# Branch gates and branch outputs as separate units of work, a shorter chain of mixers, and opening loads in another order, in a two-layer decoder trunk

## The chip, the cores and the metric

The kernel runs as one program on one core of one Trainium2 chip. The metric is the device time of one execution in microseconds (us); the kernel before takes 2546.94 us, the median of three runs. In the text PE is TensorE (matmuls), ACT is ScalarE, DVE is VectorE, POOL is GpSimd, and SP is the engine whose queue issues the DMAs. A matmul of 512 columns takes its place on PE for about 0.227 us (43.53 us for 192 in a row, in the chain of work of the profile).

## The reference, cut to what matters

512 tokens of width 1024 pass through two layers. Each layer is a half-step SwiGLU FFN, a block of four parallel token mixers, and a second half-step FFN. The block that the change touches:

```
h  = rmsnorm(x);  z = h @ w_in           # q, k, v and gates of four mixers
outs = (diff_attention, mlstm, stick_breaking, dsa)      # four mixers, each 512 x 256
y  = sum over b of sigmoid(gate_b) * (outs[b] @ w_branch[b])    # gate_b is 512 x 1024
x  = x + y @ w_out
```

`dsa` picks the 256 best keys of each query by a learned index score. `mlstm` needs input and forget gates. All is computed in float32; a product is made of three fp32r matmuls of high and low parts.

## The kernel before, in words

All tensors lie with features on the 128 partitions and the 512 tokens along the free dimension. A weight tile of 128 x 1024 is split into a high and a low part (`weights()`), and each 128 x 128 block of it multiplies a tile `xh`/`xl` of the input three times (`mm3`). A projection of one output tile is 8 blocks, so 24 matmuls of 512 columns.

The FFNs are plain loops. The mixer block (`mixers()`) is different. One long chain of small steps, `heads()`, runs the mixers one after the other: stick-breaking, the index of dsa, mlstm, differential attention, dsa. A step issues some score matmuls (tiles `S`), and ACT and DVE work on the scores. Later `weigh_steps` transposes the weights of a head (tiles `T`) and multiplies them with the values (tile `A`). Beside this chain stands a list of *units*: projections and branch units, all with many full matmuls into tiles `g`. A small planner (`run()`, `fill()`) keeps a clock of the PE work issued so far. A chain step says how long its results will take (`yield SB_US`, `yield DIFF_US` and so on); until that much PE work has been issued, the planner issues pieces of units, the first unit in the list whose `needs` are done. When no unit can go, the planner issues the next chain step at once. The scheduler of the framework then fixes one order for each engine, and each engine runs its own order strictly.

In the kernel before, `branch_unit` holds both a gate projection and the branch output that it multiplies, for two of the eight output tiles, and it needs the finished mixer (`o_sb`, `o_ml`, `o_diff`, `o_dsa`):

```
def push_branch(name, pairs, *needs):
    for i in pairs:
        push(f"{name}{i}", branch_unit(name, i), ("o_" + name, *needs))
```

The 512-wide half tiles of branch weights take a place in the same ring of three places, `w`, as the 1024-wide tiles. Weights of the sb and ml gates and branches have been split ahead and come back from DRAM as high and low parts (`w<-ig` 1 MB, `w<-br` 0.5 MB); those of diff and dsa come raw (`w_raw`) and are split on ACT and DVE when used.

At the opening, SP loads the small table, the first x tile, two whole weight tiles of the second FFN column (`w_raw`), and then the pieces `raw` of the first column.

Of the kernel before, what the change touches and what calls it, by code (L numbers as in the profile page):

```python
# [39 lines left out]
for _n, _w in (("ident", 128), ("mean", 128), ("bo32", 128), ("bo64", 128), ("cum", 128), ("cols", 12),  # L40
               ("ones", 128), ("m_qk", 128), ("m_kq", 128), ("m_strict", 128), ("sel", 1024), ("selp", 256)):
    CB[_n] = (_off, _w)
    _off += _w
# [11 lines left out]
NSMALL = _off  # L55
# [7 lines left out]
IDX_US, SB_US, DIFF_US, ML_US, DSA_US = 1.89, 2.64, 3.5, 3.96, 4.46  # L63
FIRST_US, LAST_US, WEIGH_US, NORM_US, SPREAD_US, STACK_US = 7.92, 5.41, 3.0, 2.88, 9.2, 9.84
GATE_US, SELECT_US, HALF_US, DEN_US, REST_US, KV_US, OUT_US = 0.7, 6.29, 6.75, 1.24, 8.76, 1.49, 1.0
# [5 lines left out]
GB, SB_, TB, AB = 3, 2, 2, 1  # L71
BRANCH = {"diff": 0, "ml": 1, "sb": 2, "dsa": 3}
# [3 lines left out]
def trunk_kernel(ctx, tc, xT, pos, consts, small, wgu1, wdn1, wgu2, wdn2, wia, wig, wiv, wbr, wout, out,  # L76
# [44 lines left out]

    def weights(src, n, key=None, c=0):

        with tc.high_priority(offset=WPRI):
            if key in ready:
                w = w_tile()
# [4 lines left out]
            w = w_tile()  # L131
# [55 lines left out]
    for l in range(depth):  # L187
        t = cpool.tile([P, NSMALL], F32, name=f"small{l}")
        sms.append(t)
# [22 lines left out]
    def open_sums():  # L212
        sums["pool"] = ExitStack()
        p = sums["pool"].enter_context(tc.tile_pool(name="sums", bufs=1, side="right", reuse_waits="tile"))
        sums["sum"], sums["tmp"] = [p.tile([P, T], F32, name=f"rsum{i}") for i in range(2)]
# [24 lines left out]
    def rms_rows(psum):  # L240
# [6 lines left out]
        r = cpool.tile([P, T], F32, name="rrow")  # L247
# [186 lines left out]
    def mixers(l, y, mp, kp, pp, psT, psS):  # L434
# [19 lines left out]
        tasks, units, done, unit, before = [], [], {}, [None], [None]  # L454
        issued.clear()
        live = {"z": 0, "a": 0, "o": 0, "ot": 0, "norm": 0}
# [21 lines left out]
        def fill():  # L478
            if unit[0] is None:
                u = next((u for u in units if all(n in done for n in u.needs) and (not u.z or live["z"] < 3)), None)  # L480
                if u is None:
                    return False
                units.remove(u)
                live["z"] += u.z
                unit[0] = u.gen
# [30 lines left out]
        def push(name, gen, needs=(), z=0):  # L516
            units.append(SimpleNamespace(name=name, gen=gen, needs=needs, z=z))
# [56 lines left out]
        def branch_unit(name, pair):  # L574

            b = BRANCH[name]
            for i in (2 * pair, 2 * pair + 1):
                half, n = divmod(i, 4)
                w = weights(wig[l, b * KD + i], 1024, ("ig", l, b * KD + i))
                ps = gpool.tile([P, T], F32, name="g")  # L580
                yield from proj_steps(w, ps)
                g = tmp("gate", 2)
                with tc.high_priority(offset=EVPRI):
                    tanh_half(g, ps)
                if n % 2 == 0:
                    o = 512 * (n // 2)
                    bw = weights(wbr[l, b, half, :, o:o + 512], 512, ("br", l, b, half), o)
                yield
                ps = gpool.tile([P, T], F32, name="g")
                for k in range(2):  # L590
                    mm3(ps, *bw((2 * (n % 2) + k) * P), *done["o_" + name][k], k == 0, k == 1)
                with tc.high_priority(offset=EVPRI):
                    V.scalar_tensor_tensor(g if i in started else y[i], g, 1.0, ps, op0=OP.add, op1=OP.mult)
                    if i in started:
                        (V if b == BRANCH["dsa"] else G).tensor_add(y[i], y[i], g)
# [4 lines left out]
                if i % 2 == 0:  # L600
# [3 lines left out]
        def push_branch(name, pairs, *needs):  # L604
            for i in pairs:
                push(f"{name}{i}", branch_unit(name, i), ("o_" + name, *needs))
# [190 lines left out]

        def sparse_kv(z):
# [29 lines left out]
        push_branch("sb", (0,))  # L828
        push("vm", v_unit("m"), ("o_sb",))
        push_branch("sb", (1,))  # L830
        push_branch("sb", (2,), "gated")
        push_branch("sb", (3,), "gated", "ml0")
# [4 lines left out]
        push_branch("ml", (0, 1))  # L837
        push_proj("fq1", ("diff0",), after=diff_q)
        push_proj("fk1", ("diff0",), after=diff_k)
        push_branch("ml", (2,))  # L840
# [3 lines left out]
        push_branch("ml", (3,))  # L844
        push_branch("diff", range(4))
        push_branch("dsa", range(4))
# [67 lines left out]

        def gating():
# [23 lines left out]
            yield lambda: "index" in done  # L939
# [18 lines left out]
            V.tensor_scalar(mst[:, :T], f32(selr[:, 0]), 0.0, None, op0=OP.mult)  # L958
            V.tensor_scalar(mst[:, T:], f32(selr[:, 0, :P]), 0.0, None, op0=OP.mult)
# [21 lines left out]
            V.tensor_scalar(est, f32(selr[:, 0]), 0.0, None, op0=OP.mult)  # L981
# [51 lines left out]
        def differential():  # L1033
            lamt = mp.tile([P, 4], F32, name="lamt")
            for i in range(2):
                t_ = mp.tile([P, 32], F32, name="lp", bufs=2)
                lp = sm(l, "lam")
                V.tensor_mul(t_, lp[:, 64 * i:64 * i + 32], lp[:, 64 * i + 32:64 * i + 64])
                V.reduce_sum(lamt[:, i:i + 1], t_, axis=AX.X)
            S.activation(lamt[:, :2], lamt[:, :2], AF.Exp)  # L1040
            V.tensor_sub(lamt[:, 2:3], lamt[:, 1:2], lamt[:, 0:1])
            V.tensor_scalar(lamt[:, 2:3], lamt[:, 2:3], -lam_init, None, op0=OP.add)
# [41 lines left out]
        def mlstm():  # L1084
            yield from get("gated")
            mv, mvl = yield from need("vm")
            yield lambda: not weighing
            for h in range(4):
# [5 lines left out]
                else:  # L1094
                    spawn(*((stacks(0), "stk0") if pr else (halves(("mq1", twice), ("mk1", both)), "ml1")))
# [304 lines left out]
```

## Time and profile before

| | |
|---|---|
| median of 3 runs | 2546.94 us (2545.94 to 2547.75) |
| the profiled execution | 2546.6 us, span 2544.8 us |
| PE | 98% of the span busy, 11584 matmuls |
| DVE / ACT / POOL | 58% / 39% / 6% |
| granted PE clock over the span | 0.987 of full |

The profile shows PE busy nearly always, and the share of busy time of a pipelined engine overstates its work. What can be won stands in the stretches where PE is less than full or where its granted clock is below 1. The mixer block of layer 0 lies from about 376 to 880 us, that of layer 1 from about 1640 to 2143 us. In the tables by stretch the second number in a column is the number of instructions, and PEclk is the mean granted clock of the stretch (1.00 is 2.4 GHz, 0.50 is 1.2 GHz).

### The profile page before, as it was taken

How to read it: one execution, taken by the hardware profiler on the slowest of the kernel's cores; microseconds unless marked ns; L12 is line 12 of the kernel's file. 1: busy time of each engine (PE TensorE's matmuls, PEld its weight loads, DVE VectorE, ACT ScalarE, POOL GpSimd, SP SyncE). 2: the span in 40 equal slices, each digit the busy share in tenths (PEclk: the TensorE clock that was granted, in tenths of full speed). 3: DMA queues.
4: the chain of work that ended last, by engine and by line, in shares of the span. 5: the costliest groups of instructions: out<-in, count | busy, mean ns of one | idle time of the engine just before them, and what ended most of it. 6: DMA issues, size and time to landing. Idle time of an engine off the chain costs nothing.

```text
span 2544.8 us, 30625 instructions
## 1 busy us (share of the span) xinstructions
PE 2496.6 (98%) x11584; PEld 2043.2 (80%) x11584; DVE 1481.8 (58%) x2664; ACT 983.7 (39%) x1556; POOL 154.6 (6%) x104
## 2 busy tenths in 40 slices
PE   8999999999989999999999999999999899999999
PEld 6888888778667888888888888887777678888887
DVE  7655557895465554343565655479954754444433
ACT  5434434633345332232343444345323543322222
POOL 1000010001012010000100000100011120100000
PEclk9999999999989999999999999999999899999999
DMA  8999966544521423323289999464555124232332
GB/s 293 321 324 331 334 237 205 156 152 156 168 68 63 139 93 100 99 92 99 91 311 319 339 327 330 153 224 126 176 164 165 34 80 135 96 99 93 99 99 91
DMA packets 113026, 444.11 MB, mean 175 GB/s; under 512 B 14704, under 2 KB 15984, under 8 KB 90352
## 3 DMA queue, kind: packets, MB, share of 16 engines
q1 hardware_dynamic: 112880, 442.16, 51.6%
q8 instruction: 91, 1.49, 0.2%
q14 instruction: 55, 0.45, 0.1%
HBM read 320.47 MB, written 102.76 MB: 166 GB/s over the span
## 4 chain that ended last, share of the span: by engine, by line
PE 87%; DVE 7%; DMA 2%; ACT 2%; issue 1%; POOL 0%; SPq 0%; DVEq 0%; ACTq 0%; POOLq 0%
PE g L102 43%; PE d L102 18%; PE u L102 18%; PE S L102 3%; PE A L102 1%; PE T L108 1%; DVE scores L902 1%; DMA w<-ig 1%; DVE m L901 1%; PE T L102 1%; DVE w L133 1%; DVE rl L93 0%; DMA stk<-stk 0%; DVE z L700 0%; ACT w L132 0%
## 5 line engine op out<-in xcount | busy, mean ns | idle before, releaser
L102 PE MATMUL g<-xh,w 128*128 128x512 f32 x3008 | 1001.7, 398 | 11.4 <-DMA w<-ig 5.6
L102 PEld LDWEIGHTS g<-xh,w 128*128 128x128 f32 x3008 | 570.2, 190 | 129.9 <-DVE stk L93 5.3
L132 ACT ACTIVATE w<-w_raw 128x1024 fp32r<-128x1024 f32 (+1 forms) x334 | 339.4, 1019 | 705.5 <-PE g L102 249.2
L102 PE MATMUL g<-xl,w 128*128 128x512 f32 x1504 | 594.4, 395 | 0.3 <-DVE xl L96 0.3
L133 DVE TENSOR_TENSOR w<-w_raw,w 128x1024 fp32r<-128x1024 f32 (+1 forms) x334 | 395.2, 1185 | 109.2 <-ACT w L132 109.0
L102 PE MATMUL u<-xh,w 128*128 128x512 f32 x1408 | 454.5, 390 | 0.5 <-DVE w L93 0.5
L102 PE MATMUL d<-hh,w 128*128 128x512 f32 x1408 | 435.6, 389 | 0.2 <-ACT hh L92 0.2
L102 PEld LDWEIGHTS g<-xl,w 128*128 128x128 f32 x1504 | 285.9, 190 | 56.4 <-DVE xl L96 1.1
L102 PEld LDWEIGHTS u<-xh,w 128*128 128x128 f32 x1408 | 264.6, 188 | 55.4 <-DVE w L93 0.9
L102 PEld LDWEIGHTS d<-hh,w 128*128 128x128 f32 x1408 | 264.3, 188 | 55.2 <-ACT hh L92 0.6
L102 PE MATMUL d<-hl,w 128*128 128x512 f32 x704 | 274.1, 389 | 0.2 <-DVE hl L93 0.2
L102 PE MATMUL u<-xl,w 128*128 128x512 f32 x704 | 274.1, 389 | 0.0
L171 DVE TENSOR_TENSOR a_w<-a_raw,a_w 128x1024 fp32r<-128x1024 f32 x92 | 112.5, 1223 | 112.9 <-ACT a_w L170 112.6
L337 DVE SCALAR_TENSOR_TENSOR x<-d,x 128x512 f32<-128x512 f32 x96 | 66.3, 691 | 190.3 <-PE d L102 190.3
L287 DVE TENSOR_TENSOR u<-u,rrow 128x512 f32<-128x512 f32 x88 | 60.7, 689 | 170.1 <-PE u L102 170.1
L170 ACT ACTIVATE a_w<-a_raw 128x1024 fp32r<-128x1024 f32 x92 | 97.3, 1059 | 154.9 <-DMA a_raw<-in_wig_dram 65.5
L102 PEld LDWEIGHTS d<-hl,w 128*128 128x128 f32 x704 | 132.1, 188 | 28.3 <-DVE hl L93 0.8
L102 PEld LDWEIGHTS u<-xl,w 128*128 128x128 f32 x704 | 132.4, 188 | 27.4
L225 POOL TENSOR_TENSOR rsum<-rsum,rsum 128x512 f32<-128x512 f32 x42 | 67.5, 1607 | 1234.8 <-ACT rsum L223 1234.8
L285 DVE TENSOR_TENSOR t<-g,rrow 128x512 f32<-128x512 f32 x88 | 60.7, 690 | 114.5 <-PE g L102 109.0
L102 PE MATMUL S<-stk 128*128 128x384 f32 (+3 forms) x304 | 94.0, 369 | 15.8 <-ACT p L713 8.4
L102 PE MATMUL g<-oh,w 128*128 128x512 f32 x256 | 93.6, 404 | 0.5 <-ACT gate L688 0.5
(262 smaller groups left out, 2602.7 us busy)
## 6 DMA issues: line engine op xcount, KB each, us to landing
w_raw<-in_wgu_dram SPq DMA_DIRECT2D x174, 512.0 KB, 3.8
ia<-a_w SPq DMA_DIRECT2D x40, 1024.0 KB, 6.6
w<-ia SPq DMA_DIRECT2D x40, 1024.0 KB, 5.4
w_raw<-in_wdn_dram SPq DMA_DIRECT2D x64, 512.0 KB, 4.1
ig<-a_w SPq DMA_DIRECT2D x32, 1024.0 KB, 6.9
w<-ig SPq DMA_DIRECT2D x32, 1024.0 KB, 5.9
a_raw<-in_wia_dram SPq DMA_DIRECT2D x40, 512.0 KB, 6.8
a_raw<-in_wig_dram SPq DMA_DIRECT2D x32, 512.0 KB, 7.2
```

Of the source, the lines that this page charges most:

```text
L102: ins = PE.matmul(out, a, b, start=start, stop=stop, skip_group_check=True)
L108: PE.transpose(out, a, C("ident")[p:n, p:n])
L132: S.activation(w[:, 0, :n], raw[:, :n], AF.Copy)
L133: V.tensor_sub(w[:, 1, :n], raw[:, :n], f32(w[:, 0, :n]))
L170: S.activation(w[:, 0], raw, AF.Copy)
L171: V.tensor_sub(w[:, 1], raw, f32(w[:, 0]))
L225: G.tensor_add(sums["sum"], sums["sum"], sums["tmp"])
L285: V.tensor_mul(t, pg, r)
L287: V.tensor_mul(u, pu, r)
L337: V.scalar_tensor_tensor(x[i], ps, 0.5, x[i], op0=OP.mult, op1=OP.add)
L901: V.max(out=m8, in_=s)
L902: V.match_replace(out=s, in_to_replace=m8, in_values=s, imm_value=TAKEN)
```

## The change

PE's work stays the same matmuls (one more warming matmul at the start). What changes:

- `branch_unit` becomes `gate_unit` (24 matmuls, tanh, result in a place) and `out_unit` (12 matmuls for two output tiles). A gate needs no mixer, only a place: for sb the first four go into `y`, for diff six go into the tiles of mlstm's values (`stash`), the others into a ring of four tiles `gate` (before: two). `fill()` avoids two out units in a row while another unit can go (`resting`).
- The half tiles of branch weights get a place of their own, `wb`, one tile; the three places `w` hold only 1024-wide tiles.
- The planner's numbers change (the waits after a chain step are shorter).
- The chain is shorter: `gating` no longer waits for the index, `mlstm` no longer waits at its end for its last output, the second half of mlstm's q and k is asked for at its start, and lambda of the differential attention is computed at the start of the block from a load of its own.
- At the opening the pieces of the first column are loaded before the tiles of the second, with high priority.
- Constants shrink (`sel` 1024 to 8 columns, `lam` out of the small table), and `rrow` moves to the pool of the sums.

```
-IDX_US, SB_US, DIFF_US, ML_US, DSA_US = 1.89, 2.64, 3.5, 3.96, 4.46
+IDX_US, SB_US, DIFF_US, ML_US, DSA_US = 1.5, 2.4, 3.0, 3.3, 4.0
...
+    def w_half():
+        return wpool.tile([P, 2, 512], FR, name="wb", bufs=1)
...
-                u = next((u for u in units if all(n in done for n in u.needs) and (not u.z or live["z"] < 3)), None)
-                if u is None:
+                able = [u for u in units if all(n in done for n in u.needs)
+                        and (not u.z or live["z"] < 3) and (not u.g or live["g"] < GATES)]
+                if not able:
                     return False
+                u = next((u for u in able if not (u.out and resting[0])), able[0])
...
-        def branch_unit(name, pair):
+        def gate_unit(name, i, place):
             b = BRANCH[name]
-            for i in (2 * pair, 2 * pair + 1):
...
+            w = weights(wig[l, b * KD + i], 1024, ("ig", l, b * KD + i))
+            ps = gpool.tile([P, T], F32, name="g")
+            yield from proj_steps(w, ps)
+            g = place()
+            with tc.high_priority(offset=EVPRI):
+                tanh_half(g, ps)
+            done[f"g_{name}{i}"] = g
+
+        def out_unit(name, pair, ring):
+            b = BRANCH[name]
+            half, o = pair // 2, 512 * (pair % 2)
+            bw = weights(wbr[l, b, half, :, o:o + 512], 512, ("br", l, b, half), o)
+            for n, i in enumerate((2 * pair, 2 * pair + 1)):
+                g = done[f"g_{name}{i}"]
                 ps = gpool.tile([P, T], F32, name="g")
                 for k in range(2):
-                    mm3(ps, *bw((2 * (n % 2) + k) * P), *done["o_" + name][k], k == 0, k == 1)
+                    mm3(ps, *bw((2 * n + k) * P), *done["o_" + name][k], k == 0, k == 1)
...
+        def push_gates(name, tiles, place=None, needs=()):
+            for i in tiles:
+                push(f"g_{name}{i}", gate_unit(name, i, place or (lambda: tmp("gate", GATES))), needs, g=int(not place))
...
-        push_branch("diff", range(4))
-        push_branch("dsa", range(4))
+        for p in range(3):
+            push_gates("diff", (2 * p, 2 * p + 1), stash, ("mlo1",))
+            push_outs("diff", (p,), ring=())
+        push_gates("diff", (6, 7))
+        push_outs("diff", (3,))
+        for p in range(4):
+            push_gates("dsa", (2 * p, 2 * p + 1))
+            push_outs("dsa", (p,))
...
-            yield lambda: "index" in done
             yield GATE_US
...
+            spawn(halves(("mq1", twice), ("mk1", both)), "ml1")
             yield lambda: not weighing
...
-            yield from get("mlo1")
...
-        for i in range(8):
+        for i in range(9):
             PE.matmul(ps, idle[:, :P], idle, start=True, stop=True, skip_group_check=True)
...
-    with tc.tile_pool(name="first", bufs=1, reuse_waits="tile") as rp:
+    with tc.tile_pool(name="first", bufs=1, reuse_waits="tile") as rp, tc.high_priority(offset=2 * WPRI):
```

First place: PE, layer 0, where dsa's first head starts. `S` are score tiles, `mask,identb` adds a mask, `g<-x..,w` are matmuls of a gate or projection. Before:

```order
L102 MATMUL S<-mask,identb 128x384
L102 MATMUL S<-stk 128x512 x2
L102 LDWEIGHTS identb
L102 MATMUL S<-mask,identb 128x512
L102 MATMUL S<-stk 128x128 x2
L102 LDWEIGHTS identb
L102 MATMUL S<-mqk,identb 128x128
L102 MATMUL S<-stk 128x256 x2
L102 LDWEIGHTS identb
L102 MATMUL S<-mask,identb 128x256
L102 MATMUL S<-stk 128x384 x2
L102 LDWEIGHTS identb
```

The scores of six steps stand there one right behind the other. Now, at the same scores of the same heads:

```order
L104 MATMUL S<-mqk,identb 128x128
L104 MATMUL g<-xl_82,w 128x512
L104 MATMUL g<-xh_74,w 128x512
L104 MATMUL g<-xh_75,w 128x512
L104 MATMUL g<-xl_83,w 128x512
L104 MATMUL g<-xh_75,w 128x512
L104 MATMUL S<-stk 128x256 x2
L104 LDWEIGHTS identb
L104 MATMUL S<-mask,identb 128x256
L104 MATMUL g<-xh_76,w 128x512
L104 MATMUL g<-xl_84,w 128x512
L104 MATMUL g<-xh_76,w 128x512
```

Five gate matmuls stand between the scores of one step and the next, and nine behind that.

Second place: PE, layer 0, the first two outputs of the ml branch. `oh_5543` is a finished half of the mixer's output, `w_5523` and `wb_5547`, `wb_5676` are half tiles of branch weights. Before, behind the first output of a pair:

```order
L102 MATMUL g_5610<-oh_4951,w_5523 128x512
L102 MATMUL S_5438<-stk_5269,stk_5259 128x128
L102 LDWEIGHTS identb_89
L102 MATMUL S_5438<-mqk_90,identb_89 128x128
L102 MATMUL g_5610<-ol_4952,w_5523 128x512
L102 MATMUL g_5610<-oh_4951,w_5523 128x512
L102 MATMUL g_5610<-oh_5422,w_5523 128x512
L102 MATMUL g_5610<-ol_5423,w_5523 128x512
L102 MATMUL g_5610<-oh_5422,w_5523 128x512
L102 MATMUL g_5621<-xh0_71,w_5619 128x512
```

A gate (`w_5619`) follows the last matmul with the half tile. Now:

```order
L110 MATMUL T_5534<-cst_67,tmp_5413 128x128 x4
L104 MATMUL g_5549<-oh_5543,wb_5547 128x512
L104 MATMUL g_5558<-oh_5543,wb_5547 128x512
L104 MATMUL g_5549<-ol_5544,wb_5547 128x512
L104 MATMUL g_5549<-oh_5543,wb_5547 128x512
L104 MATMUL g_5558<-ol_5544,wb_5547 128x512
L104 MATMUL g_5558<-oh_5543,wb_5547 128x512
L104 MATMUL S_5569<-stk_5293,stk_5283 128x512
L104 LDWEIGHTS identb_89
```

Right behind these nine rows come a second score step of 512 columns, eight small matmuls of tiles `T`, and then the first matmul with the next half tile, `wb_5676`, in the same single place. The four transposes at the head of the piece, which the output `oh_5543` is made from, have moved to directly ahead of it.

Third place: SP's queue at the very start. `x` are input tiles, `raw` the pieces of the first FFN column, `w_raw` the tiles of the second. Before:

```order
L1213 DMA small0_87<-in_small_dram 128x186
L1214 DMA x0_104<-in_xT_dram 128x512
L130 DMA w_raw_255<-in_wgu1_dram 128x1024
L130 DMA w_raw_260<-in_wgu1_dram 128x1024
L1231 DMA raw0_132<-in_wgu1_dram 128x256
L1231 DMA raw1_133<-in_wgu1_dram 128x256
```

The pieces come fifth and sixth, behind 1 MB of tiles. Now:

```order
L1279 DMA raw0_134<-in_wgu1_dram 128x256
L1261 DMA small0_87<-in_small_dram 128x58
L1279 DMA raw1_135<-in_wgu1_dram 128x256
L1262 DMA x0_105<-in_xT_dram 128x512
L1275 DMA x1_106<-in_xT_dram 128x512
L1275 DMA x2_107<-in_xT_dram 128x512
```

The tiles `w_raw` have moved behind the last of the x tiles, to the eighteenth place.

## Rows read from the trace of the kernel before

**Rows 1.** The page: busy time, share of the span and instructions by engine.
```profile
PE 2496.6 (98%) x11584; PEld 2043.2 (80%) x11584; DVE 1481.8 (58%) x2664; ACT 983.7 (39%) x1556; POOL 154.6 (6%) x104
```

**Rows 2.** Stretches, layer 0: length, busy PE, PEld, DVE, ACT, POOL; PEclk, DMA share, GB/s.
```profile
0.00:25.00 25.00, 19.28 (x64) 12.28 (x65) 15.87 (x20) 14.31 (x27) 8.73 (x10) 0.93 0.81 288
...
410.00:473.00 63.00, 63.00 (x364) 53.36 (x363) 47.25 (x92) 33.08 (x68) 5.21 (x3) 1.00 0.64 197
473.00:507.00 34.00, 30.98 (x192) 25.83 (x190) 32.50 (x91) 21.35 (x48) 1.08 (x3) 1.00 0.39 122
507.00:600.00 93.00, 91.53 (x447) 73.84 (x446) 79.74 (x230) 31.99 (x62) 0.00 (x0) 1.00 0.45 151
600.00:640.00 40.00, 38.68 (x184) 31.13 (x182) 23.08 (x66) 10.33 (x19) 8.88 (x6) 0.96 0.53 163
640.00:700.00 60.00, 55.43 (x257) 41.95 (x258) 31.14 (x85) 23.95 (x66) 5.51 (x4) 0.94 0.55 164
700.00:750.00 50.00, 46.50 (x231) 36.72 (x229) 33.39 (x105) 21.09 (x47) 7.52 (x5) 0.93 0.25 79
750.00:780.00 30.00, 25.67 (x118) 18.34 (x117) 22.69 (x60) 22.59 (x57) 5.54 (x4) 0.77 0.08 27
```

**Rows 3.** By stretch, the same parts of layer 1.
```profile
1736.00:1770.00 34.00, 30.96 (x191) 25.83 (x190) 32.47 (x90) 21.33 (x48) 1.08 (x3) 1.00 0.38 120
1770.00:1863.00 93.00, 91.01 (x445) 73.43 (x445) 79.42 (x228) 32.14 (x62) 0.00 (x0) 1.00 0.45 152
1863.00:1903.00 40.00, 39.10 (x186) 31.57 (x184) 23.53 (x67) 10.33 (x19) 8.92 (x6) 0.96 0.51 161
1903.00:1963.00 60.00, 55.74 (x259) 42.20 (x260) 31.69 (x86) 23.96 (x66) 5.51 (x4) 0.94 0.55 168
1963.00:2013.00 50.00, 46.72 (x228) 37.03 (x227) 33.03 (x104) 20.86 (x47) 7.41 (x5) 0.90 0.24 75
2013.00:2043.00 30.00, 25.68 (x117) 18.28 (x117) 22.73 (x60) 22.50 (x56) 5.67 (x4) 0.77 0.09 27
```

**Rows 4.** Waits of PE, 395 to 840 us: total, times, longest.
```profile
PE S L102 <- ACT p L713: 4.2, 6, 1.1
...
PE g L102 <- DMA w<-ig: 2.2, 1, 2.2
```

**Rows 5.** PE in order of time: a dsa score step and what ended its wait.
```profile
759.53 0.80 PE L102 MATMUL S<-stk 128*128 128x256 f32 x2 [1.14 <-ACT p L713]
```

**Rows 6.** By stretch, a piece inside the differential heads, columns as in rows 2.
```profile
643.50:646.90 3.40, 3.40 (x11) 2.32 (x10) 2.87 (x9) 1.53 (x6) 1.27 (x1) 0.50 0.45 103
```

**Rows 7.** Chain of waits: start, us, what.
```profile
101.96 43.53 PE d L102 x192
```

**Rows 8.** DMA issues: count, KB each, median us from issue to landing.
```profile
w<-br SPq DMA_DIRECT2D x16, 512.0 KB, 4.7
```

**Rows 9.** ACT in order of time: an output half made in layer 0.
```profile
623.16 0.63 ACT L92 ACTIVATE oh<-ot 128x512 fp32r<-128x512 f32 x1 [5.18 <-DVE ot L1140]
```

**Rows 10.** DVE in order of time: the steps ahead of that half.
```profile
621.66 0.74 DVE L628 SCALAR_TENSOR_TENSOR ot<-ot,mhg,T 128x512 f32<-128x512 f32 x1
...
622.44 0.69 DVE L1140 SCALAR_TENSOR_TENSOR ot<-z,ot 128x512 f32<-128x512 f32 x1
```

**Rows 11.** All engines in order of time: the opening.
```profile
1.18 0.42 SPq L1214 DMA_DIRECT2D x<-in_xT_dram  x1
...
1.64 0.91 SPq L130 DMA_DIRECT2D w_raw<-in_wgu_dram  x2
...
4.30 0.72 ACT L95 ACTIVATE xh<-x,small 128x512 fp32r<-128x512 f32 x1 [2.07 <-DMA x<-in_xT_dram]
...
7.60 0.42 ACT L92 ACTIVATE w<-raw 128x256 fp32r<-128x256 f32 x1 [2.05 <-DMA raw<-in_wgu_dram]
...
8.07 0.50 PE L102 MATMUL g<-xh,w 128*128 128x512 f32 x1 [3.26 <-ACT w L92]
```

More of the change, by code (lines that the diff above doesn't have):

```diff
@@ L187, in trunk_kernel @@
     for l in range(depth):
-        t = cpool.tile([P, NSMALL], F32, name=f"small{l}")
+        t = cpool.tile([P, NMAIN], F32, name=f"small{l}")
         sms.append(t)
@@ L214, in open_sums @@
         p = sums["pool"].enter_context(tc.tile_pool(name="sums", bufs=1, side="right", reuse_waits="tile"))
-        sums["sum"], sums["tmp"] = [p.tile([P, T], F32, name=f"rsum{i}") for i in range(2)]
+        sums["sum"], sums["tmp"], sums["row"] = [p.tile([P, T], F32, name=n) for n in ("rsum", "square", "rrow")]
     def epilogue(i, gain):
@@ L246, in rms_rows @@
         rsqrt_columns(ps, NT, v, y, t)
-        r = cpool.tile([P, T], F32, name="rrow")
+        r = sums["row"]
         spread(r.rearrange("p (t f) -> p t f", t=NT), y[:, :, None], P)
@@ L450, in blk @@
             return slice(i * P, i * P + n)
-        tasks, units, done, unit, before = [], [], {}, [None], [None]
+        tasks, units, done, unit, before, resting = [], [], {}, [None], [None], [False]
         issued.clear()
-        live = {"z": 0, "a": 0, "o": 0, "ot": 0, "norm": 0}
+        live = {"z": 0, "a": 0, "o": 0, "ot": 0, "norm": 0, "g": 0}
         def spawn(gen, key=None):
@@ L514, in take, with push @@
             live[what] += 1
-        def push(name, gen, needs=(), z=0):
-            units.append(SimpleNamespace(name=name, gen=gen, needs=needs, z=z))
+        def push(name, gen, needs=(), z=0, g=0, out=False):
+            units.append(SimpleNamespace(name=name, gen=gen, needs=needs, z=z, g=g, out=out))
         def proj_steps(w, ps):
@@ L594, in branch_unit @@
                     if i in started:
-                        (V if b == BRANCH["dsa"] else G).tensor_add(y[i], y[i], g)
+                        (V if name == "dsa" else G).tensor_add(y[i], y[i], g)
+                live["g"] -= i in ring
                 started.append(i)
@@ L796, in mixers @@
             V.tensor_scalar(gains[n], sm(l, n), -s / 8192, None, op0=OP.mult)
+        lamt, lp = mp.tile([P, 4], F32, name="lamt"), tmp()
+        nc.sync.dma_start(lp[:, :128], small[l, :, NMAIN:])
+        for i in range(2):
+            o = 64 * i
+            V.tensor_mul(lp[:, 128 + o:160 + o], lp[:, o:o + 32], lp[:, o + 32:o + 64])
+            V.reduce_sum(lamt[:, i:i + 1], lp[:, 128 + o:160 + o], axis=AX.X)
+        S.activation(lamt[:, :2], lamt[:, :2], AF.Exp)
+        V.tensor_sub(lamt[:, 2:3], lamt[:, 1:2], lamt[:, 0:1])
+        V.tensor_scalar(lamt[:, 2:3], lamt[:, 2:3], -lam_init, None, op0=OP.add)
         def sparse_kv(z):
@@ L827, in mixers @@
             push_proj(n, func=silu_conv(i))
-        push_branch("sb", (0,))
+        for i in range(4):
+            push_gates("sb", (i,), lambda i=i: y[i], (f"sb{i // 2}",))
+        push_outs("sb", (0,), ring=())
         push("vm", v_unit("m"), ("o_sb",))
-        push_branch("sb", (1,))
-        push_branch("sb", (2,), "gated")
-        push_branch("sb", (3,), "gated", "ml0")
+        push_gates("sb", (4, 5))
+        push_outs("sb", (1,), ring=())
+        push_gates("sb", (6, 7))
+        push_outs("sb", (2,), "gated")
+        push_outs("sb", (3,), "gated", "ml0")
         push_proj("mo0", ("ml0",), func=tanh_half)
@@ L1094, in mlstm @@
                 else:
-                    spawn(*((stacks(0), "stk0") if pr else (halves(("mq1", twice), ("mk1", both)), "ml1")))
+                    if pr:
+                        spawn(stacks(0), "stk0")
                 acc = psA()
```

77 lines of the change are left out of this document (37 added, 40 removed).

## The prediction

> **What bounds the kernel now.** I read the page first, then the table by stretch, then the waits of PE, then single places in order of time. On the page PE is busy for 98% of the span, DVE for 58%, ACT for 39% [rows 1], and the change leaves PE the same matmuls. So nothing can be won but the time in which PE has no matmul, or runs them at half clock.
>
> The tables by stretch show where that is. In a stretch of length W with PE busy B and mean granted clock c, the loss is (W - B) + (1 - c) x W: the first part is idle, the second is work that a clock at half speed (1.2 instead of 2.4 GHz) did not do. Layer 0 [rows 2]: 410 to 473 loses nothing (63.00 busy of 63.00, clock 1.00). 473 to 507 loses 3.0, with DVE busy 32.50 of 34. 507 to 600 loses 1.5; 600 to 640 loses 1.3 + 1.6 = 2.9; 640 to 700 loses 4.6 + 3.6 = 8.2; 700 to 750 loses 3.5 + 3.5 = 7.0; 750 to 780 loses 4.3 + 6.9 = 11.2. Together 33.8 us. Layer 1, the same six stretches [rows 3]: 3.0, 2.0, 2.5, 7.9, 8.3 and 11.2, together 34.9 us. The opening, 0 to 25, loses 5.7 + 1.75 = 7.5 us [rows 2]. That is 76 us in all; the FFNs lose next to nothing.
>
> Why they are lost: from 640 to 780 the chain of mixers (differential attention, then dsa) is alone or nearly alone on PE. A score step waits for the ACT exponential that frees its PSUM tile: six waits, 4.2 us in all, in layer 0 [rows 4], for example 1.14 us at 759.53 [rows 5]. The units that could stand between need `o_diff` or `o_dsa`, which the chain has yet to make. Half clock stands behind such waits, as in 643.5 to 646.9, where PE is busy all the time and the clock is 0.50 [rows 6]. One gate waits 2.2 us for its weights [rows 4], since the half tiles hold places of the ring of three.
>
> **Opening.** Now the first real matmul waits at 8.07 for the piece `raw`, which ACT gets at 7.60 although x was there at 4.30 [rows 11]: 1 MB of `w_raw` is issued ahead of it, at 1.64. The transfer of x takes 4.30 - 1.18 = 3.1 us. In the new order x is fourth; with 0.45 us for each issue (0.91 for two) it is issued at about 2.1, lands at 5.2, and ACT needs 0.72: first matmul at about 5.9, 2.2 us earlier. The nine warming matmuls end about then, so the idle gap that precedes the half clock is gone too; its price was the 1.75 us above. Then ACT sets the pace: eight `xh` at 0.66, eight halves of weights at 0.42 and five squares at 0.62 are 11.7 us behind 5.2, so about 17, and PE ends the first column's 48 matmuls near 18. At 0.227 us a matmul [rows 7] it has issued about 48 + 31 = 79 by 25 us, against 64 - 8 = 56 real ones now [rows 2]: 23 x 0.227 = 5.2 us. I take 4.5, since the second column's weights now land last and have to be split. The bounds are 0 (they are late by all that was won) and the whole loss, 7.5.
>
> **Gates ahead of the mixers.** The order now puts five to nine gate matmuls (1.1 to 2.0 us) between the score steps of dsa, where it put none. That covers a wait like the 1.14 us. Between 640 and 780 layer 0 loses 26.4 us, layer 1 27.4. I keep 6 us of it in each layer: at about eight places the new order still has two score steps within 1.5 us of each other on the same pair of PSUM tiles (half a microsecond each), and the last head's transposes stand close to their products (2 us). Bounds: 0, and all of it. I keep 1.3 us more where a head norm's transposes stand directly ahead of the first outputs of diff.
>
> **Index and gating.** Gates of sb need only finished input halves, so they fill the index steps, which took 34 us with DVE full and now have some 54 us of PE work beside them. Of 3.0 us I keep 1.0; bounds 0 and 3.0. Mlstm runs beside the selection of keys, and DVE is busy 79.74 of 93 us there. The order has about 72 us of PE work between mlstm's first and last score step, where it had 77, so DVE goes from 86% to about 92%: I put 3.0 us here against 1.5 to 2.0 now. Bounds: nothing, and DVE wholly in the way, (79.7 - 72), 7.7 us.
>
> **New waits at the ml outputs.** Here the change adds a wait. In the order the last matmul with `wb_5547` is followed by a score step of 512 columns, eight small matmuls, and the first with `wb_5676`: some 1.2 us of work. `wb` is one place, so the second load can't start before the first tile is used up, and a half tile takes 4.7 us to land [rows 8]: a wait of 3.5 us on PE. Queued behind that load on SP are seven parts of the next differential head's score operands; they come as late, but so does PE. Just ahead of it, the transposes `T_5534` are followed at once by products with `oh_5543`, which needs 0.74 + 0.69 on DVE and 0.63 on ACT first [rows 9, 10]: 2.1, with handovers 2.5 us. Together 6.0 us in each layer (bounds 0 and 8), and 2.5 us of half clock behind them, from one to two pieces as in rows 6 at 1.7 us each. At the other seven loaded half tiles of a layer the order has over 6.5 us of PE work between release and use, which covers 4.7.
>
> The Trainium skill bears on this ("Trainium Kernel Development and Optimization", Best Practices): double-buffer, so that DMA and compute overlap; one place is what it warns of. By that rule alone all sixteen loads of half tiles would wait, which would cost sixteen times 4.7, 75 us; by the cover that I count, two do. No row of the kernel before shows a ring of one.
>
> **The sum.** Left in each layer: 1.0 + 3.0 + 6.0 + 2.5 + 6 + 1.3 = 19.8 us. Won: 33.8 - 19.8 = 14.0 and 34.9 - 19.8 = 15.1, so 29.1, and 4.5 at the opening: 33.6 us. The smaller constants, `rrow`'s new home and the early lambda I put at nothing: the same few operations beside full PE work; lambda's load is issued among the weight loads ahead of the first score step, and would cost what it lands later than that. The profiled execution took 2546.6 us, 0.3 below the median of the runs. 2546.6 - 33.6 = 2513.
>
> **Rivals.**
> The filling works better: the waits of 6.0 and 2.5 don't come, and 5 us are left of the rest in each layer. For it: the loss sits almost wholly where PE had nothing else, and now it has. Against it: the two places at the ml outputs stand plainly in the order. 2546.6 - 28.8 - 29.9 - 5 = 2483.
>
> The gain is mostly eaten: PE's waits move with the chain. For it: DVE is at 95% in 473 to 507 and at 86% in mlstm, so steps that come sooner find it full, and the bounds above cost 4.7 and 2 us more in each layer; a loss of half of the 26 us between 640 and 780 (7 us more) comes with them. 33.6 - 2 x 13.7 = 6: 2540 at the far end, 2530 in the middle.
>
> Slower, by chain steps that stand too close: the planner's numbers shrink (2.64 to 2.4, 3.5 to 3.0, 3.96 to 3.3), and the order has 12 matmuls between stick-breaking steps where it had 15, 2.7 instead of 3.4 us. PE runs its order strictly, so a step whose operands are late stops everything. There are 16 + 24 + 16 + 16 + 16 = 88 steps in each layer. It decides from (33.6 + 5) / 176 = 0.22 us of wait per step; at 0.35 us the time is 2513 + 62 = 2575. Against it: in 410 to 473 DVE is busy 47 of 63 us and ACT 33 [rows 2], which leaves room for steps 18% closer, and PE has no idle there at all.
>
> Slower, by the single place at every load: 14 more loads of 4.7 us without cover are 66 us, 2579. The order's 6.5 us and more of cover speak against it.
>
> **How the numbers follow.** Forecast (2498 to 2527) 0.52; better filling (below 2498) 0.16; mostly eaten (2527 to 2541) 0.19; no change 0.05; steps too close 0.05; single place 0.03. Within 0.2%, 5.1 us, is about what a measurement of this kernel can't tell from no change. Faster: 0.52 + 0.16 + 0.19 = 0.87. Same: 0.05. Slower: 0.08. The range leaves out about one in ten at each end: 2484 to 2538.
>
> **What would show it.** In the table by stretch, the dsa part should have clock 1.00 and PE busy over 95%; the pieces at half clock should be fewer and lie where the ml outputs are. The list of PE's waits should have a DMA `wb<-br` of about 3.5 us in each layer and no `w<-ig`. The first real matmul should start near 6 us. The forecast is wrong if PE waits for `S` or `A` in the stick-breaking or mlstm stretch by more than some 4 us, if the wait for `wb` is nought, or if the dsa stretch still runs at half clock.

## The result and the profile after

The changed kernel took 2513.66 us (median of 4 runs, 2511.71 to 2517.21) against 2547.35 for the kernel before beside it: a ratio of 0.9869, interval 0.9852 to 0.9886, 33 us faster. The forecast was 2513.0, and the mechanism was the one that it named. But two of its terms are off by more than a half, in opposite directions, and cancel in the sum.

The page of the changed kernel, busy time by engine and one of the groups of matmuls (busy and mean ns; idle time ahead and what ended it), answers to [rows 1].

```profile
PE 2476.3 (99%) x11585; PEld 2028.7 (81%) x11585; DVE 1487.2 (59%) x2662; ACT 985.3 (39%) x1556; POOL 145.5 (6%) x104
...
L104 PE MATMUL g<-oh,wb 128*128 128x512 f32 x256 | 94.5, 424 | 8.0 <-ACT oh L94 4.5
```

The number of matmuls and the busy time are nearly what they were; PE's idle time and its half clock went. The products with the half tiles `wb` now stand out: 8.0 us idle ahead of 256 of them.

The table by stretch of the changed kernel (width, PE busy and instructions, granted clock, DMA share, GB/s), the opening and layer 0, answers to [rows 2]; the last row is a second, narrower question.

```profile
0.00:25.00 25.00, 21.21 (x73) 1.00 0.68 226
...
460.00:520.00 60.00, 58.86 (x326) 1.00 0.62 187
520.00:600.00 80.00, 78.63 (x389) 1.00 0.39 138
600.00:640.00 40.00, 39.16 (x191) 1.00 0.61 193
640.00:680.00 40.00, 34.37 (x155) 0.83 0.38 113
680.00:720.00 40.00, 38.70 (x203) 1.00 0.47 142
720.00:780.00 60.00, 59.53 (x301) 1.00 0.17 53
...
643.70:657.30 13.60, 11.10 (x32) 0.50 0.33 91
```

By the formula of the prediction, 720 to 780 (mostly dsa) loses 0.5 us; in the kernel before, 750 to 780 alone lost 11.2. One place is left: 640 to 680 loses 5.6 us idle and 0.17 x 40 = 6.8 us of half clock, all of it in one piece from 643.7 to 657.3. The opening has no half clock any more. Layer 1 has the same place at 1890 to 1930, against [rows 3], and a smaller loss at the start of its mixers (1650 to 1720), where the kernel before has none.

```profile
1890.00:1930.00 40.00, 34.40 (x156) 0.83 0.37 112
...
1650.00:1720.00 70.00, 67.32 (x407) 1.00 0.59 187
```

Added up over the mixers, 405 to 860 in layer 0 and 1650 to 2075 in layer 1, the losses are 12.5 + 6.8 = 19.3 and 14.6 + 6.8 = 21.4 us. The forecast left 19.8 in each, for the stretches from the index to dsa alone; there layer 0 still loses 17.5 and layer 1 18.0. Of the rest of layer 1, 2.7 us are lost at 1650 to 1720, 1.8 of them in one wait of the first stick-breaking step for its operands.

PE's waits in layer 0, 380 to 860 (total, times, longest), answer to [rows 4].

```profile
PE A L104 <- DVE rl L95: 3.8, 9, 0.7
PE g L104 <- ACT oh L94: 2.2, 1, 2.2
PE g L104 <- DMA wb<-br: 1.7, 1, 1.7
PE T L104 <- ACT tmp L645: 1.7, 2, 1.5
PE S L104 <- ACT p L743: 1.4, 2, 1.0
```

The waits of score steps for the exponential went from 4.2 to 1.4 us, and the wait for `w<-ig` is gone. Two of the new ones stand together at the outputs of mlstm. PE there (start, duration, idle time ahead and what ended it):

```profile
640.67 1.05 PE L104 MATMUL T<-cst,tmp 128*128 128x4 f32 x8 [1.51 <-ACT tmp L645]
...
644.46 1.22 PE L104 MATMUL g<-oh,wb 128*128 128x512 f32 x2 [2.24 <-ACT oh L94]
...
652.93 0.77 PE L104 MATMUL g<-oh,wb 128*128 128x512 f32 x1 [1.75 <-DMA wb<-br]
```

And SP's queue in the same stretch:

```profile
647.43 0.58 SPq L132 DMA_DIRECT2D wb<-br  x1
648.05 4.42 SPq L684 DMA_DIRECT2D stk<-stk  x7
```

The load of the second half tile is issued at 647.43, when the last matmul with the first one has gone, and PE can go on at 652.93. It was busy from 647.19 to 651.18, with two score steps and small matmuls at half clock, and then idle.

The opening, against [rows 11]: the first real matmul, and from the view by line the first `d` matmul (the down projection), a mark that all of the opening's work must precede. In the kernel before, the two stand at 8.07 and 101.80.

```profile
5.79 0.50 PE L104 MATMUL g<-xh,w 128*128 128x512 f32 x1 [0.55 <-ACT xh L97]
...
L104 PE MATMUL d<-hh,w x32: 389/389/389, 99.2 to 109.8; 128*128 128x512 f32 x32
```

So the opening won 2.6 us of the profiled execution's 31.7 (2546.6 to 2514.9). The output projection of layer 0 starts at 854.95, where it started at 873.49: 18.5 earlier, of which 2.5 were there at the start of the mixers, so layer 0 won 16.0. Layer 1 won the other 13.

### The profile page after: what moved, and what is told of

Its sections match the earlier page's. It is cut to its first block, busy times and chain, and to the rows that moved or that the text cites. A ratio compares the mean times of both kernels' runs of the same rounds, so it can differ in the third digit from the quotient of the medians.

```text
span 2513.1 us, 30534 instructions
## 1 busy us (share of the span) xinstructions
PE 2476.3 (99%) x11585; PEld 2028.7 (81%) x11585; DVE 1487.2 (59%) x2662; ACT 985.3 (39%) x1556; POOL 145.5 (6%) x104
## 4 chain that ended last, share of the span: by engine, by line
PE 76%; issue 9%; DVE 9%; DMA 4%; ACT 2%; POOL 1%; SPq 0%; DVEq 0%; ACTq 0%; POOLq 0%
PE g L104 35%; PE d L104 18%; PE u L104 18%; PE S L104 2%; DVE scores L957 2%; DVE m L956 1%; PE A L104 1%; DVE w L138 1%; DMA stk<-stk 1%; PE T L104 1%; PE T L110 1%; DMA a_raw<-in_wia_dram 1%; DMA w_raw<-in_wig_dram 1%; DVE tmp L665 0%; DVE rl L95 0%
## 5 line engine op out<-in xcount | busy, mean ns | idle before, releaser
L104 PEld LDWEIGHTS g<-xh,w 128*128 128x128 f32 x3008 | 563.5, 188 | 117.7 <-DMA w<-ia 2.1
L137 ACT ACTIVATE w<-w_raw 128x1024 fp32r<-128x1024 f32 (+1 forms) x318 | 329.1, 1036 | 686.8 <-PE g L104 233.2
L138 DVE TENSOR_TENSOR w<-w_raw,w 128x1024 fp32r<-128x1024 f32 (+1 forms) x318 | 380.2, 1197 | 111.9 <-ACT w L137 111.8
L230 POOL TENSOR_TENSOR rsum<-rsum,square 128x512 f32<-128x512 f32 x42 | 64.7, 1542 | 1244.2 <-ACT square L228 1244.2
L290 DVE TENSOR_TENSOR t<-g,rrow 128x512 f32<-128x512 f32 x88 | 60.6, 689 | 111.9 <-PE g L104 107.4
L104 PE MATMUL g<-oh,wb 128*128 128x512 f32 x256 | 94.5, 424 | 8.0 <-ACT oh L94 4.5
L104 PE MATMUL S<-stk 128*128 128x384 f32 (+3 forms) x304 | 88.4, 345 | 5.7 <-ACT p L743 3.1
```

The costliest lines, as they stand in the source:

```text
L104: ins = PE.matmul(out, a, b, start=start, stop=stop, skip_group_check=True)
L137: S.activation(w[:, 0, :n], raw[:, :n], AF.Copy)
L138: V.tensor_sub(w[:, 1, :n], raw[:, :n], f32(w[:, 0, :n]))
L230: G.tensor_add(sums["sum"], sums["sum"], sums["tmp"])
L290: V.tensor_mul(t, pg, r)
```

## The experiments

Ratios are to the kernel before. The changed kernel, run once more among these, gave 0.9885 (0.9866 to 0.9904) beside the 0.9869 of the first time. "Given back" below is counted from the middle of the two, 0.9877; 0.001 is 2.5 us.

**The changed kernel again.**

> The changed kernel without any edit, on the chip of these runs, as the base that the other runs are read against. It should repeat its ratio of 0.9869 to the kernel before, within 0.9855 to 0.9885. If it comes out at 0.985 or below, the gain of 0.0016 of the run with mlstm's second half tile in the big ring is no gain.

Measured: 2517.33 us. The base repeats within its interval, at its upper edge. Differences of 0.002 between kernels need a trace to stand on. At mlstm's outputs in layer 0 its trace has the same three waits (1.5, 2.2 and here 2.8 us, the last put down to DVE by the profile) and loses the same 6.8 us to half clock, but in two pieces with full clock between them, where the first trace has one piece:

```profile
643.40:650.00 6.60, 4.37 (x12) 0.50 0.38 122
650.20:653.40 3.20, 1.43 (x14) 1.00 0.74 225
653.60:660.20 6.60, 5.78 (x15) 0.50 0.14 35
```

**Gates tied to their mixer.**

```
- push(f"g_{name}{i}", gate_unit(...), needs, g=int(not place))
+ push(f"g_{name}{i}", gate_unit(...), ("o_" + name, *needs), g=int(not place))
```

> The changed kernel, but every gate unit needs the outputs of its mixer again, so that no gate runs ahead. Theory A (the gates are the filler): the score steps of dsa stand bare again, half clock comes back in the last 120 us of the mixers of each layer, and most of the 29 us won in the two layers goes: 2534 to 2544 us. Theory B (the planner's numbers and the shorter chain made the gain, the gates only fill what would be full anyway): under 8 us are given back, 2514 to 2522 us.

Measured: 2530.5 us, 0.9948 (0.9933 to 0.9963): 18 us given back, between the two theories and nearer to A. The table by stretch shows why it isn't all:

```profile
640.00:680.00 40.00, 39.72 (x201) 1.00 0.46 151
...
720.00:780.00 60.00, 49.10 (x227) 0.80 0.11 36
```

The dsa stretch loses 10.9 + 12.0 = 22.9 us in layer 0, where the changed kernel loses 0.5. But 640 to 680 loses 0.3, where it loses 12.4. Gates that run ahead take the filler from mlstm's outputs and bring it to dsa. They win some 22 us a layer at the one place and pay 12 at the other.

**The planner's numbers of before.**

```
-IDX_US, SB_US, DIFF_US, ML_US, DSA_US = 1.5, 2.4, 3.0, 3.3, 4.0
+IDX_US, SB_US, DIFF_US, ML_US, DSA_US = 1.89, 2.64, 3.5, 3.96, 4.46
-... SELECT_US ... = ... 2.9 ...
+... SELECT_US ... = ... 6.29 ...
```

> The changed kernel with the six planner numbers of before (1.89, 2.64, 3.5, 3.96, 4.46 and 6.29 for a round of the selection). Theory A (free gates are enough by themselves): the gates still stand between the steps, 2514 to 2520 us. Theory B (the number for the selection sets when dsa comes): 48 rounds at 6.29 are planned as 302 us instead of 139, dsa is put behind nearly all gates, its steps stand bare with half clock, and some 11 us in each layer come back, with about 2 us more at other places: 2534 to 2544 us.

Measured: 2560.6 us, 1.0062 (1.0047 to 1.0077). Slower than the kernel before, by more than either theory said. With all else of the change in place, the old numbers turn a gain of 31 us into a loss of 16. One of them, for a round of the selection of keys, is not in the lines of the change shown ahead of the prediction: it was 6.29 and is now 2.9.

```profile
780.00:825.00 45.00, 42.28 (x183) 0.92 0.24 76
825.00:860.00 35.00, 27.22 (x134) 0.95 0.04 14
```

In layer 0 the score steps of dsa now stand at 780 to 860, behind the gates, and lose 10.5 us idle and 5.4 of half clock there.

**The number for the selection alone.**

```
-... SELECT_US ... = ... 2.9 ...
+... SELECT_US ... = ... 6.29 ...
```

> The changed kernel with one planner number of before: 6.29 instead of 2.9 for a round of the selection of keys (48 rounds). The run with all six old numbers took 1.0062 of the kernel before, 1.93% (about 49 us) above the changed kernel. Theory A (this one number decides when dsa comes, and with it whether any gates are left to stand between its steps): 35 to 50 us are given back, 2545 to 2562 us. Theory B (the numbers for the steps of the other mixers share in it, by waits of PE for S and A that stand closer): 10 to 30 us, 2522 to 2542 us.

Measured: 2541.2 us, 0.9985 (0.9976 to 0.9995): 27 us given back, at the edge of theory B and short of A. This one number carries a good half of the 47, by the late dsa (780 to 860 loses 7.4 us idle and 3.2 of half clock in layer 0); for the rest the other five have to be old as well.

**The new numbers in the kernel before.** (The same lines the other way round, and nothing else.)

> The kernel before with the six new planner numbers, and nothing else of the change. Theory A (numbers help only where gates are free to fill): in the order dsa's steps come no better covered than before, and the time is within 8 us of the kernel before, 2536 to 2552 us. Theory B (dsa comes earlier, which by itself brings it beside more of the other work): 10 to 20 us are won, 2524 to 2536 us. Rival C (steps too close): slower by over 8 us, as the forecast's rival of 0.22 us a step had it.

Measured: 2542.49 us, 0.9991 (0.9979 to 1.0002). Theory A: without gates that are free to move, the numbers are worth about 2 us, perhaps none. They aren't harmful there either, which was the price of the rival "steps too close". The wait of gates for their weights stays, 3.8 us in the two layers where the kernel before has 5.6:

```profile
PE g L102 <- DMA w<-ig: 3.8, 2, 2.0
```

**Two places instead of four.**

```
-GATES = 4
+GATES = 2
```

> The changed kernel with two places for gates that run ahead instead of four. Theory A (the number of gates that may run ahead decides): in the order the eight score steps of a head of differential attention stand next to each other while no gate may start, with half clock there, and 10 to 20 us are given back, 2520 to 2531 us. Theory B (two are enough, since each pair of outputs needs two gates): within 4 us of the changed kernel, 2508 to 2515 us.

Measured: 2546.13 us, 0.9999 (0.9987 to 1.0011): the whole gain is gone, more than theory A said. PE, and SP's queue just ahead of it:

```profile
631.13 0.23 PE L104 MATMUL S<-mqk,identb 128*128 128x128 bf16 x1
638.02 0.44 PE L104 MATMUL S<-stk 128*128 128x128 f32 x1 [6.67 <-DMA stk<-stk]
```

```profile
631.26 0.33 SPq L132 DMA_DIRECT2D w<-ig  x1
631.64 12.57 SPq L684 DMA_DIRECT2D stk<-stk  x18
```

The eight score steps stand bare, as the order said. What the order did not say is the 6.67 us ahead of them: their operands, small copies, are queued on SP behind a load of gate weights that waits for PE to free a place. The load goes out at 631.26, when the last gate matmul ahead of the scores has ended, and the copies follow from 631.64. It is 6.67 of the 16 us that layer 0 loses here beyond the changed kernel, between 405 and 860. With four places that load stands elsewhere.

**The chain of mixers as before.**

```
  V.tensor_sub(ab[:, 0], gi[:, :, 0:4], ab[:, 1])
+ yield lambda: "index" in done
...
- spawn(halves(("mq1", twice), ("mk1", both)), "ml1")      (ahead of mlstm's first head)
+ spawn(... else (halves(("mq1", twice), ("mk1", both)), "ml1"))   (behind it)
...
+ yield from get("mlo1")                                     (mlstm's last line)
```

> The changed kernel with the chain of mixers as before: gating waits for the whole index stage, the second halves of mlstm are made only behind its first head, and differential waits until mlstm's outputs are done. Theory A (filling matters, not the length of the chain): the order has gates between the steps all the same, 2514 to 2524 us. Theory B (the shorter chain carries the gain): the mixers end later than their filler, 2530 to 2540 us.

Measured: 2514.53 us, 0.9881 (0.9867 to 0.9896). Theory A: the shorter chain is worth nothing that can be measured here. The profiled span is 2513.0 against 2513.1.

**The old opening in the changed kernel.**

```
-for i in range(9):     (warming matmuls)
+for i in range(8):
-with tc.tile_pool(name="first", ...) as rp, tc.high_priority(offset=2 * WPRI):
+with tc.tile_pool(name="first", ...) as rp:
```

> The changed kernel with the opening loads in the old order (two 512 KB weight loads of the next column ahead of the first pieces) and eight warming matmuls instead of nine. Theory A (the opening's part is what the traces show at the first matmul of the down projection, 101.80 against 99.19): that matmul is back at 101 to 102.5, and 2 to 3.5 us are given back, 2515 to 2518 us. Theory B (the opening is paced by the arrival of x and by DVE all the same, and what was won there came from the smaller loads of constants): the first matmul of the down projection stays below 100, and the time at 2512 to 2515 us.

Measured: 2525.87 us, 0.9925 (0.9909 to 0.9941): 12 us given back, far more than either theory. The view by line has the first `d` matmul at 107.4, 8.2 later than in the changed kernel (the kernel before has it at 101.80); the other 4 us are no more than the two times of the changed kernel differ by. PE waits for the row of the first norm:

```profile
43.46 1.12 PE L110 MATMUL s<-cst,rrow 128*128 128x128 f32 x4 [3.35 <-ACT rrow L262]
```

DVE in that stretch shows what stands in between:

```profile
37.07 0.17 DVE L241 TENSOR_TENSOR rmst<-rmsv,rmsy 128x4 f32<-128x4 f32 x1
37.15 0.70 DVE L366 SCALAR_TENSOR_TENSOR ang<-k,ang 128x512 f32<-128x512 f32 x1
```

The angles of the rotary tables have slipped between the small steps of the norm, 0.7 us behind each of 0.17, so that the norm takes 6.7 us on DVE (33.4 to 40.1), where it takes 2.1 in the changed kernel (32.2 to 34.3). So this run doesn't isolate the loads.

**The new opening in the kernel before.** (The same lines the other way round.)

> The kernel before with the new order of the opening loads and nine warming matmuls, and nothing else of the change. In the run with the old opening in the changed kernel the first matmul of the down projection came at 107.4, since DVE had the angles of the rotary tables between the steps of the first norm; in the order of this kernel the norm's steps stand together. Theory A (the opening itself is worth what the two traces showed): the first matmul of the down projection is at 99 to 99.6 instead of 101.80, the time 2 to 4 us below the kernel before. Theory B (it was worth the 8 us of that run): 6 us or more. Theory C: nothing is left, within 1 us, with that matmul above 101.

Measured: 2541.57 us, 0.9983 (0.9970 to 0.9995), and the first `d` matmul at 98.3, 3.5 us earlier than in the kernel before:

```profile
L102 PE MATMUL d<-hh,w x35: 389/389/389, 98.3 to 109.9; 128*128 128x512 f32 x35
```

Theory A, at the high end of its time: the opening by itself is worth 3 to 4 us.

**One half tile in the big ring.** Only the load for mlstm's second pair of outputs.

```
-w = w_tile() if n > 512 else w_half()
+w = w_tile() if n > 512 or ring else w_half()     (ring: name "ml", pair 1)
```

> The changed kernel, but the second half tile of mlstm's outputs goes into the ring of three big tiles instead of the single place, so that its load need not wait for the first tile's last matmul. The wait of PE for the outputs of mlstm just ahead of it (2.2 us in each layer) stays. Theory A (the single place costs its own wait, 1.7 us a layer, and keeps the clock at half behind it): the wait for the half tile there goes, the piece at half clock ends some 4 to 6 us earlier, and 6 to 12 us are won in the two layers, 2502 to 2508 us. Theory B (the half clock hangs on the wait for the outputs, and once it has begun it lasts as long as before): only the wait itself goes, 2 to 4 us, 2510 to 2512 us. Rival: the ring place taken makes a gate wait for its weights, no change.

Measured: 2507.83 us, 0.9853 (0.9838 to 0.9869), 6 us below the middle of the base, its interval touching the base's. The trace shows the mechanism of theory A in layer 0: the wait for `wb` is gone, the wait for `oh` stays at 2.2, and 640 to 680 has clock 0.96. In layer 1 the wait for `wb` is gone too, but the half clock lasts from 1886.4 to 1896.4, behind the same wait for `oh`: 5.0 us lost.

```profile
640.00:680.00 40.00, 35.18 (x168) 0.96 0.52 164
...
1886.40:1896.40 10.00, 9.58 (x30) 0.50 0.39 129
```

The edit changed more than its theories say: the wait of 1.5 us for `tmp` is gone as well, in both layers. In layer 0 the order now has some 13 gate matmuls, and not 6, between the last score step and the transposes that need `tmp`. So the 6 us belong to the place and to that move together.

**All half tiles in the ring of three.** The single place is gone, as before the change.

```
-w = w_tile() if n > 512 else w_half()
+w = w_tile()
```

> The changed kernel with every half tile in the ring of three big tiles, as before the change, so that the single place is gone. Theory A (the half tiles held places that gates needed, so that gates came late): PE waits for weights of gates as it did for 2.2 us in the kernel before, and 2 to 8 us are lost, 2512 to 2519 us. Theory B (the single place only costs its own waits): the waits for half tiles go as in the run with one of them moved, 4 to 8 us are won, 2503 to 2507 us.

Measured: 2503.63 us, 0.9831 (0.9806 to 0.9855): 12 us won, theory B and more. The stretch of mlstm's outputs in layer 0:

```profile
640.00:680.00 40.00, 35.37 (x172) 0.96 0.51 164
```

and PE in it, where the same wait for `oh` stands:

```profile
644.64 0.73 PE L104 MATMUL g<-oh,w 128*128 128x512 f32 x2 [2.24 <-ACT oh L94]
...
649.54 0.64 PE L110 MATMUL T<-cst,tmp 128*128 128x128 f32 x4
649.93 0.48 PE L104 MATMUL g<-oh,w 128*128 128x512 f32 x1
```

The next products start at 649.93, right behind the transposes and where the changed kernel waited until 652.93; and the half clock costs 0.04 x 40 = 1.6 us there, not 6.8. In layer 1 it is 3.3 us:

```profile
1887.90:1894.50 6.60, 6.60 (x24) 0.50 0.36 110
```

As in the run with one half tile moved, the wait for `tmp` is gone too, so the 12 us are not the waits for the single place alone. No gate waits for its weights in the list of waits, although the half tiles hold places in the ring again.

**Gates of diff let go earlier.**

```
- push_gates("diff", (2 * p, 2 * p + 1), stash, ("mlo1",))
+ push_gates("diff", (2 * p, 2 * p + 1), stash, ("mlv",))
...
+ done["mlv"] = True        (behind mlstm's last head)
```

> The changed kernel, but the gates of diff, which are kept in the place of mlstm's values, may start when mlstm has used those values, not only when mlstm's outputs are done. In the order three gates then stand in the dry place around the first outputs of mlstm: ahead of them, and 18 matmuls (4.1 us) between the two loads of the single half tile. Theory A (the dry place costs what the trace shows there, 5.6 us idle and 6.8 us of half clock between 640 and 680, in each layer): 18 to 25 us are won, 2489 to 2496 us. Theory B (the filler is only moved, and is missing at dsa's end, with the half clock there): 2508 to 2516 us. Between them: the half clock goes but other waits of 2 to 4 us a layer take the place, 2496 to 2505 us.

Measured: 2501.36 us, 0.9828 (0.9812 to 0.9845): 12 us won, the case between the two theories, and with the run above the fastest kernel here; both beat the kernel before and the changed one. In layer 0:

```profile
640.00:680.00 40.00, 36.95 (x182) 0.96 0.51 156
...
720.00:780.00 60.00, 57.92 (x283) 1.00 0.20 63
```

All over the mixers, 10.5 us are lost in layer 0 and 12.3 in layer 1, against 19.3 and 21.4; some 4 us of this are lost again elsewhere, at 1613 to 1620 for a wait and a piece of half clock ahead of layer 1's mixers. What took the place of the old waits is one of 2.68 us for an exponential, at 660.53 and again in layer 1 at 1903.58. DVE and POOL ahead of it:

```profile
656.42 1.37 DVE L665 TENSOR_TENSOR tmp<-tmp,sin 128x512 f32<-128x512 f32 x1
...
658.18 1.28 DVE L666 TENSOR_TENSOR z<-z,tmp 128x512 f32<-128x512 f32 x1
```

```profile
655.96 1.29 POOL L664 TENSOR_TENSOR z<-z,cos 128x512 f32<-128x512 f32 x1 [3.77 <-DVE epss L1110]
657.20 1.72 POOL L608 TENSOR_TENSOR y<-y,gate 128x512 f32<-128x512 f32 x1
```

DVE's additions and products of two SBUF tiles take 1.3 us here, each begun while an operation of POOL runs, and the maximum that the exponential needs is queued behind them. A little earlier, DVE and then POOL:

```profile
646.90 1.28 DVE L242 TENSOR_TENSOR hnu<-hnu,hnr 128x16 f32<-128x16 f32 x1
650.35 0.69 DVE L665 TENSOR_TENSOR tmp<-tmp,sin 128x512 f32<-128x512 f32 x1
```

```profile
646.86 1.29 POOL L608 TENSOR_TENSOR y<-y,gate 128x512 f32<-128x512 f32 x1 [1.86 <-DVE hnu L241]
650.45 1.74 POOL L664 TENSOR_TENSOR z<-z,cos 128x512 f32<-128x512 f32 x1 [2.30 <-ACT tmp L262]
```

At 650.35 the same `tmp<-tmp,sin` took 0.69 us. POOL worked beside it there too, but began later, and took 1.74 us instead of 1.29. At 646.90 POOL was first, and an operation of 128x16, 0.18 us elsewhere, took 1.28. The two winning edits weren't run together, and the collision wasn't tested by a run of its own.

## Why the prediction came out right, term by term

**Gates ahead of the mixers: right.** This was the central step, and the runs carry it. Tied gates give back 18 us, two places all of the gain, and old numbers more than all. The dsa part runs at clock 1.00 and over 95% busy, as the last section of the prediction asked. But three parts of the edit make the gain only together: the numbers alone are worth about 2 us, free gates with old numbers lose 16. The forecast had the planner's numbers only as a danger, in the rival "steps too close", and by themselves they are next to nothing; that dsa is covered at all hangs on them, above all on the one for the selection. The prediction read the finished order, which holds both, and so it did not have to know this.

**Diff and dsa: too much kept.** 6 + 1.3 = 7.3 us a layer were left there; 600 to 640 and 680 to 780 lose 0.8 + 1.3 + 0.5 = 2.6 in layer 0. The half microseconds at "about eight places" mostly did not come: score steps wait for the exponential only twice, 1.4 us in all. No run shows why.

**Ml outputs: too little.** The forecast had 6.0 of waits and 2.5 of half clock. The waits were named rightly: 2.2 us for `oh` (forecast 2.5) and 1.7 for `wb` (forecast 3.5: the load took 5.5 us to land and not 4.7, but the cover, put at 1.2 us, lasted 4.0 at half clock). A third was not named: 1.5 us for the squares `tmp` just ahead of the norm. The three make up nearly all of the 5.6 us idle. The half clock was the mis-sized term: 6.8 us in each layer and not 2.5. The forecast took one to two pieces of 3.4 us; the two traces of the changed kernel have one of 13.6, or two of some 6.8. How much of this hangs on the second wait stays open: with the waits for `wb` and `tmp` both gone, the two runs with half tiles in the ring lose 1.6 us to half clock in layer 0, but 5.0 and 3.3 in layer 1, behind the same wait of 2.2 us for `oh`.

These 3.9 us too few (12.4 for 8.5) are outweighed by the 4.7 us too many of the paragraph above and 1.5 too many for the index and mlstm. That is why layer 0 won 16.0 for 14.0 forecast. Layer 1 won 13.0 for 15.1: its stick-breaking steps lost 2.7 us, for which the forecast had nothing. That the sum came within 1 us of the measured time is luck; the mechanism and the places are not.

**The single place: right on where it hurts, not needed for what it gives.** Two loads of sixteen waited, as counted. The prediction said that one gate of the kernel before waited 2.2 us because half tiles hold places of the ring of three [rows 4]. That fits the runs with tied gates: with the ring (new numbers in the kernel before) gates wait 3.8 us, with the single place (tied gates in the changed kernel) none does. But with gates that run ahead none waits with the ring either. So either is enough, and beside free gates the single place only costs: some 12 us by the runs, the clock and the wait for `tmp` included. The rule that the prediction weighed, in the Trainium skill ("Trainium Kernel Development and Optimization", Best Practices), to double-buffer so that DMA and compute overlap, is borne out in its direction. By it alone 75 us would have been lost; two exposed loads out of sixteen lost at most about a sixth of that.

**Index and mlstm: right or a little too much.** 460 to 520 loses 1.1 us (kept: 1.0). 520 to 600 loses 1.4 (kept: 3.0) although DVE is at 97% there; no run shows why it costs so little.

**Opening: half.** 2.6 us in the changed kernel, 3.5 in the kernel before, for 4.5 forecast. The first matmul came when it should (5.79, forecast 5.9), and the half clock went. But by 25 us PE has issued 73 - 9 = 64 real matmuls and not 79, and the second column starts at 21.9 and not near 18. ACT stands idle for 1.09 us until 8.17, when the third tile of x is there, and behind the first matmul PE's waits are for DVE's splits `xl` and `w`:

```profile
8.17 0.72 ACT L97 ACTIVATE xh<-x,small 128x512 fp32r<-128x512 f32 x1 [1.09 <-DMA x<-in_xT_dram]
```

```profile
PE g L104 <- DVE xl L98: 1.0, 2, 0.6
PE u L104 <- DVE w L95: 0.5, 1, 0.5
```

"ACT sets the pace" was the step that failed.

**The rivals.** "Steps too close" is refuted for the kernel before by the run with the new numbers in it: 0.9991. In the changed kernel layer 0 loses 1.4 us at 405 to 460 (stick-breaking) and 1.4 at 520 to 600 (mlstm), where the prediction named more than some 4 us of waits as a sign of it. "Better filling" (2483) was not reached by the change, but each of the two last edits went some 12 of the 30 us to it. "The single place at every load" did not come.

## What to carry to other kernels

Filler that may move, the places that it may move into, and the numbers that tell a planner when the chain comes are one change: taking away any one of the three cost from half of the gain to more than all of it. A wait on PE costs more than its length when half clock comes with it: 1.6 to 5.0 us behind one wait of 2.2 us here, and 6.8 where two others stood beside it. One short piece for each wait is the low end of that term. And look at what stands ahead in each queue that issues transfers: a small copy behind a load that waits for a place comes as late as that place.

## What the runs showed of the hardware that was not expected

DVE and POOL hold each other up, and the one that starts first is not slowed. DVE's operations on two SBUF operands took 1.28 and 1.37 us when an operation of POOL on SBUF tiles was under way as they began, and 0.69 us when DVE began first; then POOL's took 1.74 us instead of 1.29. One of 128x16, begun 0.04 us behind POOL's of 1.29 us, took 1.28 instead of 0.18: what it lost was the time that POOL had left.

The half clock behind a wait has no fixed length. Behind the same wait of 2.2 us, with the two others gone, PE lost 1.6, 1.6, 3.3 and 5.0 us in four places of two runs. With a wait of 1.5 us ahead of it and one of 1.7 to 2.8 us behind it, PE lost 6.8 us in layer 0 of both traces of the changed kernel, once in one piece and once in two.
